# Encoder layer, one core: element-wise sums of the Strassen-Winograd products moved from GpSimd to VectorE, and one pair of steps swapped

## The chip, the cores and the metric

One core of one Trainium2 chip runs the whole program. The metric is the device time of one execution in microseconds (us); lower is better. All arithmetic that matters here is float32; each matmul operand is split into a rounded high part and a low part, and three matmuls (high x high, high x low, low x high) stand for one float32 product.

## The reference

One encoder layer on x (1024 tokens x 1024): a SwiGLU feed-forward block (1024 -> 2 x 2816 -> 1024) as a half step, a mixing block (multi-head latent attention and grouped-query attention, 8 heads each), a second SwiGLU feed-forward block, and a last RMSNorm; scales and shifts come from a vector c through w_ada. The change lies in the two feed-forward blocks:

```
def swiglu(h, w_gu, w_down):
    a, b = jnp.split(h @ w_gu, 2, axis=-1)
    return (jax.nn.silu(a) * b) @ w_down
...
h = modulate(rms_norm(x, g_ffn1[l]), sh_f1, sc_f1)
x = x + 0.5 * gt_f1[:, None, :] * swiglu(h, w1_gu[l], w1_down[l])
```

## The kernel before

The program goes through feed-forward 1 (about 0 to 730 us), attention (to about 1300), the output projection (to about 1390) and feed-forward 2 (to the end). In each feed-forward block h @ w_gu is done by a Strassen-Winograd scheme with seven block products in place of eight. The activations are cut into B11, B21, B12, B22 and their combinations T1 to T4 (`build`, L464); the weights of a unit u of 22 are cut into A11, A12, A22 and their combinations S1 to S4 (`unit_specs`, L416). `prod` (L479) is one block product: 12 matmuls, lines L485, L486 and L487 by turns.

The weights come as a stream (`Stream`, L52): SyncE loads a 1 MB tile `raw` (two buffers); S1 and S3 are made on GpSimd from it (L426), S2 and S4 on VectorE (L426 too); then each block is split: ScalarE makes the high part `uh` (L105), VectorE subtracts it for the low part `ul` (L106). Nine split blocks may be live (`ring`). `pump` (L131) does the next steps of the stream, `get` those that a product needs.

`early2` (feed-forward 2; `early`, L571, does it for 1) and `early_rest` (L550) compute A11 x B11 and then A12 x B21 for units 0 to 7 ahead, since these need no T; between them `builds` makes the T's: eight steps of `build`, in which GpSimd makes T1's first and T3's difference (L468, L473), VectorE the other differences (L470, L476), ScalarE the high parts (L461), and VectorE (T1, T2, T3) or GpSimd (B22, T4) the low parts (L462). A11's product is copied out of its PSUM bank by ScalarE (`c`, L493) before A12's product is added in the same bank.

`run` (L614) then goes through the 22 units, five products for each of the units 0 to 7 and seven for the others. `post` (L495) takes a product out of PSUM on VectorE (L501, L507, L508), with silu on ScalarE, and `g_out` (L512) forms the blocks of g for the down product: the sums S3, S1, S2 and S4 of g on GpSimd (L521), and writes them to DRAM, the A blocks from SyncE's queue and the S blocks from GpSimd's (L517). Behind the last unit the pools are given back, and SyncE loads the gate (L397), x or z (L990, L1610) and the g blocks of the down product (raw<-g_A, L95). In units of feed-forward 1 VectorE also accumulates w_ada (`ada_use`, L313).

The code gives an order by calls; the build then orders each engine's instructions itself by what it reckons to be ready, within data dependences. L313, which the code reaches from unit 8 on, starts at 122.0 us in the trace, between the units 1 and 2. Each engine runs its queue in that order, and waits in it.

Of the kernel before, what the change touches and what calls it, by code (L numbers as in the profile page):

```python
# [19 lines left out]
ALU = mybir.AluOpType  # L20
# [31 lines left out]
class Stream:  # L52
# [87 lines left out]
    def get(self, key):  # L140
        while key not in self.units:
            assert self.i <= self.where[key], key
            if self._next_is_block() and self.live >= RING:
                self.live -= self.freed
                self.freed = 0
                assert self.live < RING, key
            self._step()
        return self.units[key]
# [35 lines left out]
def encoder_layer(ctx: ExitStack, tc: tile.TileContext, a: dict, out: bass.AP):  # L184
    nc = tc.nc
# [10 lines left out]
    st = Stream(nc, rawp, ring)  # L196
# [20 lines left out]
    def small(n, name):  # L217
        return sm.tile([P, 16], F32, tag="small", name=name, bufs=20)[:, 0:n]
# [61 lines left out]
    def ps1():  # L280

        if banks["pair"] is not None:
            p = banks["pair"][:, 512:1024]
            banks["pair"] = None
            return p
        kind = banks["kinds"][banks["n"] % len(banks["kinds"])]
        banks["n"] += 1
        if kind[0] == "2":
            p = ps2()
            if kind == "2":  # L290
                banks["pair"] = p
            return p[:, 0:512]
        return (p0p if kind == "0" else p1p).tile([P, 512], F32, tag="ps1", name="ps1")
# [122 lines left out]
    def unit_specs(i, u, early):  # L416

        src = a[f"w{i}_gu"][u // 2, u % 2]
        A = [slice(j * 512, (j + 1) * 512) for j in range(4)]
        tmps = {}  # L420

        def comb(nm, eng, x, y, op):
            def f(raw):
                tmps[nm] = sp.tile([P, 512], F32, tag="S", name="S")
                get = lambda v: tmps[v] if isinstance(v, str) else raw[:, A[v]]
                eng.tensor_tensor(tmps[nm], get(x), get(y), op=op)  # L426
            return f

        def blk(nm, v):
            if isinstance(v, str):  # L430
                return ((i, u, nm), None, lambda raw: tmps[v])
            return ((i, u, nm), A[v], None)

        direct = not early
        steps = [comb("S1", nc.gpsimd, 2, 3, ALU.add), comb("S3", nc.gpsimd, 0, 2, ALU.subtract)]
        if direct:
            steps.append(blk("A11", 0))
        steps += [comb("S2", nc.vector, "S1", 0, ALU.subtract), blk("S2", "S2"), blk("S1", "S1"), blk("S3", "S3")]
        if direct:
            steps.append(blk("A12", 1))  # L440
        steps += [comb("S4", nc.vector, 1, "S2", ALU.subtract), blk("S4", "S4"), blk("A22", 3)]
        return [(src, steps)]
# [3 lines left out]
    class GateUp:  # L446
# [17 lines left out]
        def build(self, hf, kk, part):  # L464

            b11, b21, b12, b22 = hf[0][:, kk, :], hf[0][:, kk + 4, :], hf[1][:, kk, :], hf[1][:, kk + 4, :]
            if part == 0:
                nc.gpsimd.tensor_tensor(b11, b12, b11, op=ALU.subtract)  # L468
                self.split_b("T1", kk, b11, nc.vector)
                nc.vector.tensor_tensor(b11, b22, b11, op=ALU.subtract)  # L470
                self.split_b("T2", kk, b11, nc.vector)
            else:
                nc.gpsimd.tensor_tensor(b12, b22, b12, op=ALU.subtract)  # L473
                self.split_b("T3", kk, b12, nc.vector)
                self.split_b("B22", kk, b22, nc.gpsimd)
                nc.vector.tensor_tensor(b21, b21, b11, op=ALU.subtract)  # L476
                self.split_b("T4", kk, b21, nc.gpsimd)

        def prod(self, p, u, wn, bn, kks, start, stop):  # L479
            wh, wl = st.get((self.i, u, wn))  # L480
# [31 lines left out]
        def g_out(self, fp, nm):  # L512

            g = self.g

            def put(nm):
                (nc.sync if nm[0] == "A" else nc.gpsimd).dma_start(g_d[nm][:, fp, :], g[nm])  # L517

            def comb(nm, x, y, op, into=None):
                g[nm] = gtp["g"]() if into is None else g[into]  # L520
                nc.gpsimd.tensor_tensor(g[nm], g[x], g[y], op=op)  # L521
                put(nm)

            if nm != "A21":
                put(nm)
            if nm == "A11":
                comb("S3", "A11", "A21", ALU.subtract)
            if nm == "A22":
                comb("S1", "A21", "A22", ALU.add, "A21")
                comb("S2", "S1", "A11", ALU.subtract, "A11")  # L530
                comb("S4", "A12", "S2", ALU.subtract, "A12")
# [18 lines left out]
        def early_rest(self, builds):  # L550

            K4 = (0, 1, 2, 3)
            for u0 in range(NQ0, NE, 4):
                us = range(u0, u0 + 4)
                for u in us:
                    self.bank[u] = ps1()
                    self.prod(self.bank[u], u, "A11", "B11", K4, True, True)
                    self.store_p1(u)
                    next(builds, None)
                    st.pump(2)  # L560
                    bg.step()
                for u in us:
                    self.prod(self.bank[u], u, "A12", "B21", K4, False, True)
                    self.early_out(u)
                    next(builds, None)
                    st.pump(2)
                    bg.step()
            for _ in builds:
                pass
# [96 lines left out]
    def gu_specs(i):  # L666
        for u in range(NU):
            for src, steps in unit_specs(i, u, "rest" if u < NE else None):
                st.add(src, steps)
# [191 lines left out]
    x = [xs.tile([P, D], F32, name=f"x{t}") for t in range(NT)]  # L861
# [121 lines left out]
    x = [dp.tile([P, D], F32, name=f"x{t}") for t in range(NT)]  # L983
# [439 lines left out]
    for s in range(NQ + LAG + 3):  # L1423
        if s < NQ:
            i, t = divmod(s, NT)
            p = scores(i, t)
            nm = small(1, "nm")
            nc.vector.tensor_reduce(nm, p, axis=AX.X, op=ALU.max, negate=True)  # L1428
        b = s - LAG
        if 0 <= b < NQ:  # L1430
            g, e = divmod(b, 2)
# [50 lines left out]
    oT, x, hf = {}, {}, {}  # L1482
# [120 lines left out]
    x = [dp.tile([P, D], F32, name=f"z{t}") for t in range(NT)]  # L1603
# [127 lines left out]
```

## Time and profile before

| | us |
|---|---|
| median of 3 runs | 2048.51 (2046.16 to 2048.94) |
| profiled execution | 2049.28 |
| its span, first to last instruction | 2047.5 |
| TensorE matmul busy in it | 1971.7 (96%), mean granted clock 0.988 |
| VectorE busy | 1540.1 (75%) |
| ScalarE busy | 973.4 (48%) |
| GpSimd busy | 483.7 (24%), 428 instructions |

The profiled execution has its own time, 1.8 us above its span; terms of a sum are taken from its rows. PE stands for TensorE's matmuls, DVE for VectorE, ACT for ScalarE, POOL for GpSimd, SP for SyncE; L106 is line 106 of the kernel before. An arrow in brackets behind a row names what ended the idle time before it.

### The profile page before, as it was taken

What the parts mean: (1) busy time and instruction counts of PE and PEld (TensorE: products, weight loads), DVE (VectorE), ACT (ScalarE), POOL (GpSimd) and SP (SyncE); (2) the same over time, 40 slices, a digit from 0 to 9 for tenths busy, and PEclk for the clock granted to TensorE, in tenths of its full rate; (3) what the DMA queues carried; (4) which work ended last, traced back from release to release, by engine and by line L of the source; (5) the groups of instructions that cost most, each with busy time, mean ns of one, the idle gap of its engine ahead of it and who ended that gap; (6) DMA issues with size and microseconds to landing.
All of it is one profiled execution on the core that took longest, in us unless ns stands there. A gap on an engine that the chain in (4) does not pass through costs nothing. (4 is left out here: it accounts for less than half of the span.)

```text
span 2047.5 us, 28023 instructions
## 1 busy us (share of the span) xinstructions
PE 1971.7 (96%) x10301; PEld 1678.1 (82%) x10301; DVE 1540.1 (75%) x2381; ACT 973.4 (48%) x1865; POOL 483.7 (24%) x428
## 2 busy tenths in 40 slices
PE   6889999999999999999999999998999999999998
PEld 5678888887788888798989998996788888877886
DVE  7898689886697776788888778667776555547976
ACT  6522322322344653677787777467323333324444
POOL 1544344433000032212200000005343332320011
PEclk9999999999999999999999999998999999999999
DMA  8275366565832334523253330433442332358223
GB/s 344 88 246 186 106 202 216 197 223 187 334 116 93 147 123 143 156 63 118 89 165 83 83 75 30 164 127 126 165 163 100 113 118 83 113 207 322 98 93 118
DMA packets 90550, 303.30 MB, mean 148 GB/s; under 512 B 9848, under 2 KB 22427, under 8 KB 76588
## 3 DMA queue, kind: packets, MB, share of 16 engines
q1 hardware_dynamic: 81018, 274.21, 39.8%
q0 software_dynamic: 7040, 23.07, 2.9%
q10 hardware_dynamic: 2354, 4.22, 0.5%
q8 instruction: 81, 1.33, 0.3%
q14 instruction: 57, 0.47, 0.1%
HBM read 220.98 MB, written 80.49 MB: 147 GB/s over the span
## 5 line engine op out<-in xcount | busy, mean ns | idle before, releaser
L105 ACT CAST uh<-raw 128x512 fp32r<-128x512 f32 (+1 forms) x343 | 210.4, 622 | 228.8 <-PE ps L486 148.1
L106 DVE TENSOR_TENSOR ul<-raw,uh 128x512 fp32r<-128x512 f32 (+1 forms) x343 | 250.3, 735 | 41.1 <-ACT uh L105 40.7
L105 ACT CAST uh<-S 128x512 fp32r<-128x512 f32 x198 | 121.6, 621 | 302.3 <-PE ps L486 234.7
L741 PE MATMUL ps<-uh 128*128 128x512 f32 x616 | 240.8, 393 | 7.3 <-ACT uh L105 7.3
L742 PE MATMUL ps<-ul,uh 128*128 128x512 f32 x616 | 241.5, 392 | 1.7 <-DVE ul L106 1.7
L743 PE MATMUL ps<-uh,ul 128*128 128x512 f32 x616 | 240.9, 391 | 0.0
L1428 DVE TENSOR_REDUCE nm<-ps 128x1 f32<-128x1024 f32 x128 | 155.7, 1216 | 70.6 <-PE ps L223 40.9
L106 DVE TENSOR_TENSOR ul<-S,uh 128x512 fp32r<-128x512 f32 x198 | 168.8, 858 | 41.8 <-ACT uh L105 41.6
L521 POOL TENSOR_TENSOR g<-g 128x512 f32<-128x512 f32 x88 | 135.1, 1535 | 244.3 <-DVE g L508 243.3
L1446 ACT CAST ph<-ps 128x512 fp32r<-128x512 f32 x256 | 138.0, 590 | 79.6 <-PE ps L1445 79.4
L426 POOL TENSOR_TENSOR S<-raw 128x512 f32<-128x512 f32 x88 | 123.4, 1414 | 200.3 <-DMA raw<-in_w_gu_dram 122.5
L1456 DVE TENSOR_TENSOR pl<-ps,ph 128x512 fp32r<-128x512 f32 x256 | 163.9, 683 | 0.0
L1451 ACT ACTIVATE pe<-ps,nm 128x1024 f32<-128x1024 f32 x128 | 143.6, 1122 | 17.2 <-DVE nm L1428 17.1
L741 PEld LDWEIGHTS ps<-uh 128*128 128x128 f32 x616 | 116.1, 189 | 33.2 <-ACT uh L105 9.0
L742 PEld LDWEIGHTS ps<-ul,uh 128*128 128x128 f32 x616 | 116.4, 189 | 27.7 <-DVE ul L106 3.8
L743 PEld LDWEIGHTS ps<-uh,ul 128*128 128x128 f32 x616 | 116.3, 189 | 24.2
L1445 PE MATMUL ps<-ident,pe 128*128 128x128 f32 x1024 | 134.9, 273 | 0.8 <-DVE pl L1456 0.4
L1445 PEld LDWEIGHTS ps<-ident,pe 128*128 128x128 f32 x1024 | 119.7, 141 | 19.0 <-DVE pl L1456 0.6
L105 ACT CAST uh<-hT 128x512 fp32r<-128x512 f32 x96 | 59.7, 622 | 150.4 <-PE ps L742 113.5
L1394 PE MATMUL po<-ph,V 128*128 128x256 f32 x512 | 129.7, 291 | 0.0
L1395 PE MATMUL po<-pl,V 128*128 128x256 f32 x512 | 125.9, 283 | 0.0
L233 POOL TENSOR_TENSOR r<-v,neghalf 128x1 f32<-128x1 f32 x32 | 26.0, 813 | 363.8 <-DVE v L229 363.8
(280 smaller groups left out, 5178.0 us busy)
## 6 DMA issues: line engine op xcount, KB each, us to landing
raw<-in_w_gu_dram SPq DMA_DIRECT2D x52, 1024.0 KB
ada<-in_w_ada_dram SPq DMA_DIRECT2D x56, 512.0 KB
g_S<-g POOLq DMA_DIRECT2D x88, 256.0 KB, 2.6
g_A<-g SPq DMA_DIRECT2D x66, 256.0 KB
hT<-in_w_down_dram SPq DMA_DIRECT2D x16, 1024.0 KB
raw<-g_S SPq DMA_DIRECT2D x16, 1024.0 KB
raw<-g_A SPq DMA_DIRECT2D x12, 1024.0 KB
x<-in_x_dram SPq DMA_DIRECT2D x16, 512.0 KB
```

The costliest lines, as they stand in the source:

```text
L105: nc.scalar.copy(hi[:, 0:n], ap)
L106: nc.vector.tensor_tensor(lo[:, 0:n], ap, f32(hi[:, 0:n]), op=ALU.subtract)
L521: nc.gpsimd.tensor_tensor(g[nm], g[x], g[y], op=op)
L741: nc.tensor.matmul(p, gh[:, tsl], wh, start=start, stop=False, skip_group_check=True)
L742: nc.tensor.matmul(p, gh[:, tsl], wl, start=False, stop=False, skip_group_check=True)
L743: nc.tensor.matmul(p, gl[:, tsl], wh, start=False, stop=stop, skip_group_check=True)
L1394: nc.tensor.matmul(po[:, 0:256], V, gr.ph[:, k, :], start=(k == 0), stop=False)
L1428: nc.vector.tensor_reduce(nm, p, axis=AX.X, op=ALU.max, negate=True)
L1445: nc.tensor.transpose(out=pt[:, k, :], in_=pe[:, (4 * n + k) * P:(4 * n + k + 1) * P], identity=ident)
L1446: nc.scalar.copy(gr.ph[:, 4 * n:4 * n + 4, es], pt)
L1451: nc.scalar.activation(pe, p, AF.Exp, bias=nm, accum_out=ls[:, s % 2:s % 2 + 1])
L1456: nc.vector.tensor_tensor(gr.pl[:, nsl, es], pts[n], f32(gr.ph[:, nsl, es]), op=ALU.subtract)
```

## The change

The sums S1 and S3 of the weights, the differences L468 and L473 and the low parts of B22 and T4 in `build`, and the four sums of g in `g_out` are issued on VectorE in place of GpSimd. In `early_rest`, two steps of the weight stream (`pump(2)`) are called ahead of a step of `builds` in place of behind it. GpSimd keeps the DMA issues of g's S blocks (L517).

```diff
@@ -432,7 +432,7 @@
-        steps = [comb("S1", nc.gpsimd, 2, 3, ALU.add), comb("S3", nc.gpsimd, 0, 2, ALU.subtract)]
+        steps = [comb("S1", nc.vector, 2, 3, ALU.add), comb("S3", nc.vector, 0, 2, ALU.subtract)]
@@ -465,16 +465,16 @@
             if part == 0:
-                nc.gpsimd.tensor_tensor(b11, b12, b11, op=ALU.subtract)
+                nc.vector.tensor_tensor(b11, b12, b11, op=ALU.subtract)
                 self.split_b("T1", kk, b11, nc.vector)
...
             else:
-                nc.gpsimd.tensor_tensor(b12, b22, b12, op=ALU.subtract)
+                nc.vector.tensor_tensor(b12, b22, b12, op=ALU.subtract)
                 self.split_b("T3", kk, b12, nc.vector)
-                self.split_b("B22", kk, b22, nc.gpsimd)
+                self.split_b("B22", kk, b22, nc.vector)
                 nc.vector.tensor_tensor(b21, b21, b11, op=ALU.subtract)
-                self.split_b("T4", kk, b21, nc.gpsimd)
+                self.split_b("T4", kk, b21, nc.vector)
@@ -518,7 +518,7 @@
                 g[nm] = gtp["g"]() if into is None else g[into]
-                nc.gpsimd.tensor_tensor(g[nm], g[x], g[y], op=op)
+                nc.vector.tensor_tensor(g[nm], g[x], g[y], op=op)
                 put(nm)
@@ -556,14 +556,14 @@
                     self.store_p1(u)
+                    st.pump(2)
                     next(builds, None)
-                    st.pump(2)
                     bg.step()
...
                     self.early_out(u)
+                    st.pump(2)
                     next(builds, None)
-                    st.pump(2)
                     bg.step()
```

## Rows read from the trace of the kernel before

**Rows 1.** The page, part 1: busy time of each engine.
```profile
PE 1971.7 (96%) x10301; PEld 1678.1 (82%) x10301; DVE 1540.1 (75%) x2381; ACT 973.4 (48%) x1865; POOL 483.7 (24%) x428
```

**Rows 2.** Windows, undisturbed stretch: us, busy (instructions) of PE, PEld, DVE, ACT, POOL, clock, DMA, GB/s.
```profile
1450.00:1500.00 50.00, 50.00 (x222) 41.38 (x222) 36.97 (x49) 15.30 (x25) 18.72 (x16) 1.00 0.46 158
```

**Rows 3.** Waits of PE, whole program: us in total, times, longest.
```profile
PE ps L741 <- ACT uh L105: 7.3, 4, 3.3
PE ps L485 <- ACT c L493: 6.8, 2, 6.2
...
PE ps L487 <- DVE ul L106: 5.7, 3, 3.9
PE ps L485 <- DVE s L501: 4.1, 1, 4.1
```

**Rows 4.** Timelines of DVE, then POOL, in feed-forward 2's early stretch: start, duration, line.
```profile
1398.25 2.65 DVE L106 TENSOR_TENSOR ul<-raw,uh 128x512 fp32r<-128x512 f32 x2 [9.02 <-ACT uh L105]
...
1407.63 0.68 DVE L462 TENSOR_TENSOR T2l<-hT,T2h 128x512 fp32r<-128x512 f32 x1
1408.23 0.68 DVE L462 TENSOR_TENSOR T1l<-hT,T1h 128x512 fp32r<-128x512 f32 x1
...
1411.48 1.79 DVE L106 TENSOR_TENSOR ul<-raw,uh 128x512 fp32r<-128x512 f32 x1
...
1394.86 5.50 POOL L468 TENSOR_TENSOR hT<-hT 128x512 f32<-128x512 f32 x4 [6.41 <-ACT hT L374]
...
1411.05 3.38 POOL L426 TENSOR_TENSOR S<-raw 128x512 f32<-128x512 f32 x2 [3.89 <-DMA raw<-in_w_gu_dram]
```

**Rows 5.** Lines L426 on POOL and L313 on DVE: ns min/median/max, first and last start.
```profile
L426 POOL TENSOR_TENSOR S<-raw x88: 1268/1294/2271, 89.4 to 1767.9; 128x512 f32<-128x512 f32 x88
...
L313 DVE SCALAR_TENSOR_TENSOR acc<-ada,cact,acc x56: 1269/1277/2916, 122.0 to 469.7; 128x1024 f32<-128x1024 f32 x56
```

**Rows 6.** Windows of three stretches, columns as in rows 2.
```profile
100.00:152.00 52.00, 45.60 (x189) 36.65 (x189) 47.21 (x56) 13.51 (x24) 22.71 (x19) 0.94 0.72 248
...
300.00:470.00 170.00, 170.00 (x770) 140.42 (x769) 148.35 (x175) 50.62 (x86) 69.53 (x54) 1.00 0.63 212
...
1396.00:1446.00 50.00, 39.66 (x152) 30.96 (x151) 44.51 (x43) 26.38 (x50) 32.78 (x22) 0.86 0.35 121
```

**Rows 7.** DVE's L313, groups of 108 to 165 us and of 300 to 470 us.
```profile
L313 DVE SCALAR_TENSOR_TENSOR acc<-ada,cact,acc 128x1024 f32<-128x1024 f32 x8 | 12.8, 1594 | 0.0
...
L313 DVE SCALAR_TENSOR_TENSOR acc<-ada,cact,acc 128x1024 f32<-128x1024 f32 x39 | 55.4, 1421 | 8.7 <-DMA ada<-in_w_ada_dram 8.7
```

**Rows 8.** Chain that ended last, end of feed-forward 2's units: start, duration.
```profile
1822.88 1.67 POOL g L521
...
1829.57 3.46 DMA g_S<-g
1833.36 0.33 SPq L397
...
1835.84 10.50 DMA raw<-g_A
```

**Rows 9.** Windows of PE behind it: us, PE busy (instructions), clock, DMA share, GB/s.
```profile
1844.00:1846.00 2.00, 0.30 (x2) 1.00 1.00 411
1846.00:1848.00 2.00, 0.38 (x1) 1.00 1.03 430
1848.00:1850.00 2.00, 1.69 (x6) 0.71 0.38 156
1850.00:1852.00 2.00, 2.00 (x6) 0.50 0.55 102
```

**Rows 10.** Waits of POOL and DVE; then landing of L517's DMAs.
```profile
POOL S L426 <- DMA raw<-in_w_gu_dram: 122.5, 18, 11.7
...
DVE S L426 <- POOL S L426: 17.0, 10, 3.1
...
DMA to landing us min/median/max: 2.3/2.6/8.1
```

## The prediction

> **What bounds the kernel now.** The page comes first: TensorE is busy 96% of the span, VectorE 75%, GpSimd 24% [rows 1]. So only time in which TensorE stands, or runs at the lower clock, can be won. The windows say where that is. An undisturbed 50 us hold 222 matmuls, 0.225 us each [rows 2]. The early stretch of feed-forward 2 holds 152 in 50 us, so 70 x 0.225 = 15.8 us are missing there, and the first units of feed-forward 1 hold 189 in 52 us where 231 would fit, 9.5 us missing; VectorE is busy 89% and 91% of these stretches [rows 6]. The list of waits names what TensorE stood for: low parts of weights (ul, 5.7 us in three waits), the copies c that ScalarE makes (6.8), s of VectorE (4.1), and high parts at the start of the down products (7.3) [rows 3]. Last I read the timelines of the two engines side by side: two operations of VectorE behind each other start 0.60 us apart and take 0.68 each, but one that meets a GpSimd operation takes 1.79 [rows 4]. A GpSimd operation of the same shape takes 1.29 us at the median [rows 5]. GpSimd's help is thus dear: it takes 1.3 us and may cost VectorE 1.1 us, to save VectorE 0.60.
>
> **The price of a moved operation.** 0.60 us of VectorE's queue in place of 0 to 1.11 us (1.79 - 0.68) of standing still. The 1.11 of the row is the most that I book for one. The Trainium skill (SBUF — State Buffer, section "SBUF: two separate sides") says that of two such instructions the later blocks for all of the earlier one. Taken for every instruction, it would put VectorE's time in feed-forward 2's early stretch at 25.8 + 32.8 = 58.6 us of 50, and the gain of that stretch near the whole 15.8; the row of the stretch has 44.5, so the trace does not agree to that extent, and I go by the row.
>
> **Part by part.**
>
> *Feed-forward 2's early stretch, 1396 to 1446 us.* VectorE's 43 operations would take 43 x 0.60 = 25.8 us undisturbed and take 44.5 [rows 6]. The 22 of GpSimd, all moved, add 13.2: 39.0, so 5.5 us less. VectorE also stood 9.02 us until 1398.25, while GpSimd made the four L468 from 1394.86 on [rows 4]; these now start on VectorE itself, 3.4 us earlier. Together 8.9 us in a stretch where VectorE is the engine that is late: c waits in ScalarE's queue behind high parts of T that wait for VectorE's differences. TensorE can win no more than the 15.8 us missing, and nothing if the new order puts the T's in front of what it needs next. I take **-8** (0 to -15.8), near the sum of the rows.
>
> *Feed-forward 1's early stretch, up to 100 us.* Here the swap counts: a unit's weight split gets its place ahead of the T's, on ScalarE and VectorE alike. It aims at the three waits for ul, 5.7 us, and at the slow clock behind them, about 1.0 us by what follows a like gap [rows 3, 9]. The T's pushed behind have the remaining early products to be ready in; if that cover is gone, the start of the units waits for T2 instead. I take **-6** (0 to -6.7), near the far end, since both edits act on the same three waits.
>
> *Feed-forward 1's first units, 100 to 152 us.* At most 8 of the 56 VectorE operations are L313, 1.2 us apart when undisturbed [rows 5, 7]: 8 x 1.2 + 48 x 0.60 = 38.4. Of GpSimd's 19, four DMA issues and a memset stay; 14 moved ones add 8.4: 46.8 us, against 47.2 now [rows 6]. VectorE wins nothing in sum, only the waits of its sums for GpSimd's (3.1 us at the most in one) [rows 10]. I take **-2**; bounds -9.5 (all that is missing) and +5 (VectorE at its limit, four more L313 put in its gaps).
>
> *The two ends of the units.* Behind the last g, three sums run on GpSimd one after another with a DMA issue between, from 1822.88; the last DMA of them starts at 1829.57 and takes 3.46 us; only then do SyncE's loads go out at 1833.36, and behind these the g blocks, which land at 1846.3 [rows 8]. From 1844 to 1852 us TensorE does 15 matmuls where 35.5 fit, 20.5 x 0.225 = 4.6 us: it stands 1.7 + 1.6 + 0.3 = 3.6, then runs at the lower of its two levels (0.50, that is 1.2 GHz; 6 matmuls in 2 us), which costs the other 1.0 [rows 9]. On VectorE the three sums take 1.8 us, 3.6 if a low part is put behind each, so the last DMA starts about 1826.3, 3.3 us earlier. That moves the loads by up to as much; the DMA engines were still at work then, so I count 3.0, nearly the standing time. The end of feed-forward 1 has the same pattern. The three sums also stand in front of the first low parts of the down product: +1.8 us there, against up to 3.3 (three times 1.11) of meetings gone. S2 and S4 of g also overwrite A11 and A12, whose DMAs on SyncE's queue must have read them: on VectorE a late one would now hold those low parts, GpSimd's sums did so at most from 1822.88 on, and I book nothing for it but the lower bound. I take **-6** for both ends (0 to -9.2).
>
> *The remaining units.* From 300 to 470 us VectorE would need 39 x 1.2 + 136 x 0.60 + 33 x 0.60 = 148.2 us (54 of GpSimd less 17 DMA issues and 4 memsets) where it now takes 148.4 of 170 [rows 6, 7]; TensorE is full there. In feed-forward 2's units there is no L313 and more room [rows 2]. What hides the moved work is this room and the nine live blocks of weights. I take **+1** (0 to +6, for posts that come behind the three sums of g).
>
> Sum: -8 - 6 - 2 - 6 + 1 = -21. Against the profiled execution's 2049.3 that is 2028.3; I forecast **2028 us**. That execution lies 0.8 us above the median of 2048.5, which I do not correct for.
>
> **The rivals.**
>
> *VectorE stays the limit.* By the sums above it saves 5.5 us in one stretch and nothing in another, so gains by order alone may be lost to the next late operation: the start of the units, or ScalarE's casts in their queue. Then the two ends and half of the -8 stay, and the ul waits come back elsewhere: 2049.3 - 10 + 1 = 2040. For it speaks that VectorE was already full beside GpSimd; against it, that the waits named are short and few.
>
> *VectorE waits for loads (slower).* GpSimd stood 122.5 us in 18 waits for raw tiles, 6.8 each [rows 10], with nothing useful behind it. On VectorE everything stands behind such a wait: U, s, g, low parts. A unit of five products lasts 13.5 us (60 matmuls) and holds some 17.5 VectorE operations after the move, 10.5 us, so 3.0 are free. If S1 stands 5 us each time, 2.0 us are lost 18 times: 36 us, 2049.3 - 21 + 36 = 2064. It decides from 3.0 + 21/18 = 4.2 us of standing per wait. Against it: S2, on VectorE already, needs the same tile through S1, and stood only 17.0 us in ten waits.
>
> *The S blocks of g go out late.* The DMAs that GpSimd still issues may be held up when VectorE hardly pauses. Today they land in 2.6 us at the median, 8.1 at the most. With 8.1 for the last one the loads would start at 1834.4, later than now: the ends give nothing, 2034. The Trainium skill (SBUF — State Buffer, the same section, its box on DVE and DMA) says that GpSimd cannot write descriptors while VectorE holds the ports they share. The box's case is a copy on both ports, and no run here shows it for sums of two inputs.
>
> **How the numbers follow.** Chances: forecast 0.62, VectorE the limit 0.18, late blocks 0.07, waits for loads 0.13. Cases within 0.2% (4 us, about what a measurement of this kernel can tell from no change) are a third of the second. So faster 0.81, same 0.06, slower 0.13. The bounds of the terms add up to -41 and +11, and do not all fall together; the range takes the forecast with some two thirds of the way down, and up to the limit case with its own play: 2013 to 2045. It leaves out the third rival and the worst of the second.
>
> **What would show it.** Right: no VectorE operation of 128x512 near 1.8 us in the gate-up stretches; the waits PE <- ul and PE <- c shorter; more than 170 matmuls in the 50 us from where T1 starts; L397 some 3 us closer to the last g. Wrong: a row "DVE S <- DMA raw" of tens of us, with PE <- s or g behind it; or VectorE full and TensorE's gaps only moved to the first units; or more L313 among these.

## The result, and the profile after

The kernel after takes 2003.53 us, the median of four runs (2002.6 to 2004.7); the kernel before took 2048.73 us beside it (four runs, 2046.16 to 2049.21). The ratio is 0.9782, with a 95% interval of 0.9765 to 0.9799. The gain is 45 us where 21 were forecast, and the time lies 9.5 us below the lower end of the range. The sign held, and so did the main mechanism, that VectorE and GpSimd hold each other up; the sizes did not, and at the two ends of the units the gain came another way.

The span of the profiled execution fell from 2047.5 to 2000.5 us. Part 1 of the page of the kernel after, which answers to [rows 1]:

```profile
PE 1954.1 (98%) x10301; PEld 1670.9 (84%) x10301; DVE 1554.1 (78%) x2589; ACT 975.0 (49%) x1865; POOL 172.0 (9%) x220
```

VectorE has 208 instructions more. At 0.68 us each they would be 141 us of busy time, yet its sum rose by 14 only: the operations that were there before became shorter. TensorE's busy sum fell with the same 10301 matmuls; its mean granted clock rose from 0.988 to 0.992.

Windows of the kernel after, columns as in [rows 2]. The stretches are those of [rows 6], moved by what had been won ahead of them:

```profile
88.00:140.00 52.00, 51.76 (x228) 42.91 (x229) 50.35 (x79) 17.52 (x31) 3.33 (x5) 1.00 0.67 226
...
280.00:450.00 170.00, 170.00 (x771) 140.67 (x770) 149.97 (x210) 51.43 (x87) 13.03 (x21) 1.00 0.63 213
...
1371.00:1421.00 50.00, 50.00 (x223) 41.34 (x222) 48.81 (x82) 31.41 (x59) 0.00 (x0) 1.00 0.46 158
```

In the early stretch of feed-forward 2, TensorE does 223 matmuls in 50 us instead of 152, and its clock is 1.00 instead of 0.86. The first units of feed-forward 1 hold 228 of the 231 that fit in 52 us. VectorE is 97 to 98% busy there, and TensorE stands for it nowhere in the feed-forward 2 window. VectorE does 82 instructions in the 50 us; before, VectorE's 43 and GpSimd's 22 were 65 together.

The first groups in the list of TensorE's waits after (us in total, times, longest), against [rows 3]:

```profile
PE ps L882 <- DVE v L229: 7.2, 2, 4.3
PE ps L882 <- DVE xn L875: 3.1, 2, 1.6
PE ps L485 <- ACT B11h L461: 3.0, 1, 3.0
...
PE ps L485 <- DVE s L501: 1.9, 1, 1.9
...
PE ps L741 <- ACT uh L105: 0.6, 2, 0.4
```

The waits for the weights' low parts and for c are gone, that for s has halved, and the one at the start of the down products went from 7.3 to 0.6 us. Of the 35.5 us of waits that are left, 20.2 lie in the first 60 us of the program, which the change hardly touches.

L426 in the kernel after (ns min/median/max, first and last start), and what it waited for on VectorE:

```profile
L426 DVE TENSOR_TENSOR S<-raw x88: 679/691/694, 79.4 to 1727.0; 128x512 f32<-128x512 f32 x88
...
DVE S L426 <- DMA raw<-in_w_gu_dram: 16.9, 15, 4.6
```

The longest of 88 sums takes 0.694 us. GpSimd's took 1.29 at the median [rows 5], and VectorE's operations up to 1.79 beside them [rows 4].

To say where the 47 us of span were won, I cut it at starts and ends of TensorE's work: the first product with T2, the first down product, the first input projection of the mixing block, the last output projection, the last product with T4, the last down product. Each number is the length of a section, or, from the second row on, the difference to before in us:

| kernel | to first T2 product | FFN 1 units | FFN 1 down | mixing | FFN 2 gate-up | FFN 2 down |
|---|---|---|---|---|---|---|
| before, length | 98.9 | 399.1 | 221.4 | 661.5 | 439.1 | 217.0 |
| after | -10.7 | -8.1 | -6.2 | +0.1 | -16.0 | -6.8 |
| order alone | -2.9 | +1.6 | -1.3 | +0.1 | -0.1 | +0.2 |
| T alone | -9.4 | -0.9 | -2.6 | +0.1 | -14.8 | +1.0 |
| S alone | +1.6 | -4.7 | -0.5 | +0.1 | -4.3 | -0.2 |
| g alone | +1.6 | -4.2 | -6.1 | 0.0 | +0.3 | -6.8 |

The four rows below "after" are the experiments that follow. Differences of one or two microseconds between single executions carry no weight.

### The profile page after: what moved, and what is told of

The parts are those of the page before. It is cut to its first block, busy times and chain, and to the rows that moved or that the text cites. A ratio compares the mean times of both kernels' runs of the same rounds, so it can differ in the third digit from the quotient of the medians.

```text
span 2000.5 us, 27923 instructions
## 1 busy us (share of the span) xinstructions
PE 1954.1 (98%) x10301; PEld 1670.9 (84%) x10301; DVE 1554.1 (78%) x2589; ACT 975.0 (49%) x1865; POOL 172.0 (9%) x220
## 5 line engine op out<-in xcount | busy, mean ns | idle before, releaser
L106 DVE TENSOR_TENSOR ul<-raw,uh 128x512 fp32r<-128x512 f32 (+1 forms) x343 | 235.4, 692 | 31.5 <-ACT uh L105 31.2
L106 DVE TENSOR_TENSOR ul<-S,uh 128x512 fp32r<-128x512 f32 x198 | 134.5, 684 | 34.4 <-ACT uh L105 34.4
L517 POOL DMA_DIRECT2D g_S<-g x88 | 47.9, 545 | 668.8 <-DVE g L521 597.9
L1394 PEld LDWEIGHTS po<-ph,V 128*128 128x128 f32 x512 | 97.5, 190 | 2.1
L1395 PEld LDWEIGHTS po<-pl,V 128*128 128x128 f32 x512 | 97.8, 191 | 0.2
```

The lines of the kernel that those rows point to most:

```text
L106: nc.vector.tensor_tensor(lo[:, 0:n], ap, f32(hi[:, 0:n]), op=ALU.subtract)
L1394: nc.tensor.matmul(po[:, 0:256], V, gr.ph[:, k, :], start=(k == 0), stop=False)
L1395: nc.tensor.matmul(po[:, 0:256], V, gr.pl[:, k, :], start=False, stop=(k == NT - 1))
```

## Experiments: each part of the change by itself

Four kernels, each the kernel before with one part of the change. Each was compared with the kernel before on the same chip (2047.8 us).

**The order alone**, in both early loops:

```diff
-                    next(builds, None)
                     st.pump(2)
+                    next(builds, None)
                     bg.step()
```

> The kernel before with the swap alone; every sum stays on GpSimd. Theory (VectorE stood behind GpSimd's operations; where these are gone TensorE does not wait): VectorE still meets GpSimd, so of the 45 us only the share that comes from late weight blocks in the early stretches can come: 2 to 6 us faster, about 2045, all of it ahead of the first T2 product. Rival (the new order alone does it): 10 us or more faster, below 2039.

Measured: 2047.51 us, ratio 1.0001 (0.999 to 1.0012). That is under the 2 us that the theory gave at least, and the order is worth nothing that can be told from noise: 1.6 of the 2.9 us at the first T2 product are lost again by the end of the units, and the rest is less than single executions of this kernel differ by.

**T alone:** L468, L473 and the low parts of B22 and T4 on VectorE.

```diff
-                nc.gpsimd.tensor_tensor(b11, b12, b11, op=ALU.subtract)
+                nc.vector.tensor_tensor(b11, b12, b11, op=ALU.subtract)
...
-                self.split_b("T4", kk, b21, nc.gpsimd)
+                self.split_b("T4", kk, b21, nc.vector)
```

> The kernel before with the differences and low parts of the T's on VectorE; S1, S3 and g's sums stay on GpSimd, no swap. Theory: the 26 us that the changed kernel wins ahead of the first T2 product (10.1) and in feed-forward 2's gate-up part (16.0) come mostly from here: 12 to 20 us faster, about 2033, nothing at the two ends of the units. Rival (parts don't add up, order decides): under 6 us.

Measured: 2023.15 us, ratio 0.9878 (0.9857 to 0.9899): 25 us, more than the theory gave (12 to 20) and over half of the whole gain, nearly all of it where the T's are made (-9.4 and -14.8). These are few instructions: 32 of the 208 moved.

**S alone:** S1 and S3 of the weights.

```diff
-        steps = [comb("S1", nc.gpsimd, 2, 3, ALU.add), comb("S3", nc.gpsimd, 0, 2, ALU.subtract)]
+        steps = [comb("S1", nc.vector, 2, 3, ALU.add), comb("S3", nc.vector, 0, 2, ALU.subtract)]
```

> The kernel before with S1 and S3 of the weights on VectorE alone. Theory: the first units of feed-forward 1 and the start of the units in feed-forward 2 win, 4 to 10 us in all, about 2042; VectorE's waits for raw tiles stay under 20 us. Rival (VectorE waits for loads): slower than before, over 2050, with such waits of tens of us.

Measured: 2043.67 us, ratio 0.9975 (0.9964 to 0.9986), 5 us. VectorE waited for raw tiles 22.9 us in 19 waits, 1.2 us each, far from the 4.2 at which the slower rival decides.

**g alone:** the sums of g's blocks.

```diff
-                nc.gpsimd.tensor_tensor(g[nm], g[x], g[y], op=op)
+                nc.vector.tensor_tensor(g[nm], g[x], g[y], op=op)
```

> The kernel before with the four sums of g on VectorE alone. Theory: the two ends of the units win what the changed kernel wins there, 6.2 and 6.7 us from the first down product on, so 10 to 15 us, about 2036, and little ahead of it. Rival (the ends won by the order of SyncE's loads, which the other moves made): under 4 us, and the last load of A12's blocks still behind the gate in SyncE's queue.

Measured: 2034.11 us, ratio 0.9936 (0.9919 to 0.9952): 13 us of span at the two ends, as the whole change has there. The gains of the four by ratio (0, 25, 5 and 13 us) sum to 43 of the 45 us, so the parts add up.

## Experiments: are the meetings the cause?

T and S could have won for either of two reasons: VectorE and GpSimd hold each other up, or a chain of steps is quicker on one engine. Two kernels test the first. Both are the kernel after, with extra work on GpSimd beside each of the 120 T and S operations that had moved; nothing takes its result, and both give up one of six scratch tiles for it. The first makes a sum of the same operands:

```diff
+    def beside(x, y):
+        nc.gpsimd.tensor_tensor(dmy, x, y, op=ALU.add)
...
                 self.split_b("T4", kk, b21, nc.vector)
+                beside(b21, f32(self.Bh["T4", kk]))
```

> The kernel after, and beside each weight sum (S1, S3) and each T operation that came over to VectorE GpSimd makes an extra 128x512 sum of the same operands into a tile that nobody reads; no data waits on it (a block's buffer comes free only when GpSimd has read it too). One of the scratch tiles of the norms is given up for its output. Blocking theory (VectorE's and GpSimd's two-input operations hold each other up; most of the 45 us came from those meetings): VectorE's operations beside GpSimd's sums take about 1.8 us again in place of 0.68, and since VectorE keeps the added work too, most of the 30 us that T's and S's gave are lost: 2025 to 2060 us. Rival (the gain came from the chain being on one engine, without handing over to GpSimd whose operation takes 1.28 us and without its queue): the extra sums are on no chain, 2001 to 2009 us.

The second, the control, fills the same tile and reads one column:

```diff
+        nc.gpsimd.memset(dmy, 0.0)
+        nc.gpsimd.tensor_tensor(dmy[:, 0:1], x[:, 0:1], y[:, 0:1], op=ALU.add)
```

> The control of the run before: in place of each extra sum GpSimd fills the same tile with zeros (128x512, no operand to read) and reads one column of the two operands. Both theories: GpSimd is about as busy, reads next to nothing, and the time stays within 5 us of the kernel after (2000 to 2009 us), with VectorE's 128x512 operations near 0.68 us. If it lost as much as the extra sums do, it would be GpSimd's holding the blocks, or its writes, and not its reading beside VectorE.

Measured: 2058.5 us with the sums, ratio to before 1.0057 (1.0042 to 1.0072), and 2007.52 us with the fills, ratio 0.9807 (0.979 to 0.9823). The sums cost 51 us more than the fills. Against the kernel after, the execution with the sums is 15.9 us later at the first T2 product, 20.0 longer in feed-forward 1's units and 20.6 in feed-forward 2's gate-up part; both down parts are within 0.1 us. That is where the added sums are, and nowhere else.

The longest wait of TensorE in the gate-up parts, with the sums, then with the fills, is the one in front of the first T2 product (us in total, times, longest):

```profile
PE ps L496 <- issue: 14.4, 1, 14.4
```

```profile
PE ps L497 <- POOL dmy L200: 3.9, 1, 3.9
```

For the 14.4 us the profile names no releaser ("issue"); the 3.9 it puts down to a fill. So some 10 of the 51 us may come from the place of the extra instructions in the queues and not from slower operations of VectorE. Another 5 are VectorE standing until GpSimd had read a block (3.9 and 1.2 us). The rest, about 35 us, is still more than the 30 that T and S won together. The meetings alone are thus enough for that gain; what a shorter chain adds to it was not separated.

The low parts of T4 in the kernel with the sums, then with the fills (ns min/median/max, first and last start):

```profile
L469 DVE TENSOR_TENSOR T4l<-hT,T4h x4: 683/1754/1778, 1429.4 to 1451.2; 128x512 fp32r<-128x512 f32 x4
```

```profile
L470 DVE TENSOR_TENSOR T4l<-hT,T4h x4: 684/685/689, 1391.3 to 1404.0; 128x512 fp32r<-128x512 f32 x4
```

Timelines of the kernel with the sums in this stretch, VectorE, then GpSimd (start, duration):

```profile
1427.04 0.68 DVE L478 TENSOR_TENSOR hT<-hT 128x512 f32<-128x512 f32 x1
...
1430.05 0.68 DVE L519 TENSOR_TENSOR eg<-ps,es 128x512 f32<-128x512 f32 x1
1430.65 1.17 DVE L106 TENSOR_TENSOR ul<-raw,uh 128x512 fp32r<-128x512 f32 x1
1431.74 1.78 DVE L469 TENSOR_TENSOR T3l<-hT,T3h 128x512 fp32r<-128x512 f32 x1
1433.44 1.77 DVE L469 TENSOR_TENSOR B22l<-hT,B22h 128x512 fp32r<-128x512 f32 x1
1435.13 1.74 DVE L486 TENSOR_TENSOR hT<-hT 128x512 f32<-128x512 f32 x1
1436.80 0.68 DVE L469 TENSOR_TENSOR T3l<-hT,T3h 128x512 fp32r<-128x512 f32 x1
...
1426.62 4.65 POOL L200 TENSOR_TENSOR dmy<-hT,B22h 128x512 f32<-128x512 f32 x1 [10.88 <-DVE ul L106]
1431.34 1.63 POOL L200 TENSOR_TENSOR dmy<-hT,T4h 128x512 f32<-128x512 f32 x1
1433.05 1.61 POOL L200 TENSOR_TENSOR dmy<-hT 128x512 f32<-128x512 f32 x1
1434.74 1.59 POOL L200 TENSOR_TENSOR dmy<-hT,B22h 128x512 f32<-128x512 f32 x1
```

From 1431.7 on the two engines take turns: VectorE starts an operation every 1.69 us and GpSimd one every 1.70. A pair costs 1.70 us; VectorE alone would make both in 2 x 0.60 = 1.20, by its undisturbed spacing. Where both have work, GpSimd's help thus makes the pair slower than VectorE is by itself. The Trainium skill (SBUF — State Buffer, section "SBUF: two separate sides") says that of two such instructions the first to start shuts the other out for its whole length, and only where GpSimd's reads SBUF. These rows, and the control beside them, agree.

Windows of the 50 us that begin 15 us after the mixing block's last product, in the kernel with the sums, then with the fills:

```profile
1407.00:1457.00 50.00, 37.13 (x144) 28.76 (x144) 48.82 (x51) 23.93 (x45) 34.84 (x20) 0.90 0.27 95
```

```profile
1374.00:1424.00 50.00, 48.62 (x211) 38.99 (x210) 44.69 (x74) 30.34 (x57) 21.51 (x35) 1.00 0.46 158
```

VectorE is busy 48.8 us of 50 with 51 instructions in the one, and 44.7 us with 74 in the other. TensorE does 144 matmuls against 211.

**The order, undone in the kernel after** (a weight's split behind the T's again):

```diff
-                    st.pump(2)
                     next(builds, None)
+                    st.pump(2)
                     bg.step()
```

> The kernel after without the change of order in the early units (a weight's split comes behind the T's again); all sums and low parts on VectorE. By the runs of the parts (the order alone gave nothing, the parts sum to 43 of 45 us): 2002 to 2007 us. Rival (with the T's on VectorE the order decides who waits: the T's come first in VectorE's queue and TensorE waits for the weight's low part): 2008 to 2016 us, with the first T2 product some us later or earlier.

Measured: 2002.15 us (2001.57 to 2002.89), ratio 0.9781 (0.9766 to 0.9795): no difference that this measurement can tell from the kernel after. The order is worth nothing with the T's on VectorE either.

## Experiment: what won the two ends

The gate's load (L397) was to go out some 3 us closer to the last g. SyncE's queue at the end of feed-forward 2's units, in the kernel before, then after:

```profile
1833.36 0.33 SPq L397 DMA_DIRECT2D gate<-gd  x1
1833.74 1.99 SPq L1610 DMA_DIRECT2D z<-xd  x4
1835.84 1.11 SPq L95 DMA_DIRECT2D raw<-g_A  x2
```

```profile
1786.74 0.33 SPq L95 DMA_DIRECT2D raw<-g_A  x1
1793.52 0.33 SPq L397 DMA_DIRECT2D gate<-gd  x1
1793.90 1.96 SPq L1610 DMA_DIRECT2D z<-xd  x4
```

The gate did not come closer: it stands 11.3 us behind the start of the last L508 before (1822.1) and 12.3 after (1781.2). Its wait in both kernels is for the S blocks of g. The last DMA of these, before, then after:

```profile
L517 POOL DMA_DIRECT2D g_S<-g x1: 557/557/557, 1829.6 to 1829.6; - x1
...
DMA to landing us min/median/max: 3.5/3.5/3.5
```

```profile
L517 POOL DMA_DIRECT2D g_S<-g x1: 539/539/539, 1785.9 to 1785.9; - x1
...
DMA to landing us min/median/max: 7.4/7.4/7.4
```

The sums did come out sooner: this DMA starts 4.7 us behind the start of the last L508, 7.5 before. But it takes 3.9 us longer to land, and the gate's load goes out when it has landed (1833.0 and 1793.3). Why it took longer was not tried.

The gain came by another load: one of g's blocks now stands ahead of the gate. It starts 7.6 us behind the start of the last product with T4 (1779.1), where before the first started 15.8 us behind (1820.0). The diff doesn't touch these lines; the order on SyncE's queue came out differently when the kernel was built. The end of feed-forward 1 has the same: raw at 485.63 and gate at 491.34 after, gate at 511.43 and raw at 513.89 before. Every kernel here with g's sums on VectorE has the load ahead, the one with g alone too; the kernels with the order, T or S alone have it behind.

So I took the kernel before and moved nothing but loads, at the end of both feed-forward blocks (the cut shows the first), with every sum and low part where it was:

```diff
-    gate = bcast_row(dp, gd[0], "gate")
+    gate = bcast_row(dp, gd[0], "gate", nc.gpsimd)
...
-            nc.sync.dma_start(x[t], a["x"][t * P:(t + 1) * P, :])
+            nc.gpsimd.dma_start(x[t], a["x"][t * P:(t + 1) * P, :])
```

> The kernel before, with the gate's load and the eight loads of x (or z) at the end of each FFN put on GpSimd's queue, so that on SyncE's queue the last blocks of g and the down weights no longer stand behind them; sums, low parts and the early units' order as before. Theory (the two ends were won by the order of SyncE's loads): the first product of the unit after the gate-up part no longer waits for its weight (7.3 us before), each end gives 4 to 7 us, 2034 to 2041 us. Rival (the ends were won by g's sums coming out sooner on VectorE): 2045 to 2049 us.

Measured: 2040.9 us, ratio 0.9969 (0.9958 to 0.9981), just inside what the theory gave. The down parts take 5.1 and 4.7 us less, against 6.2 and 6.8 in the kernel after, and the 7.3 us of waits at their start are down to 0.4. SyncE's queue and a window of TensorE in this kernel:

```profile
1818.41 0.49 SPq L86 DMA_DIRECT2D hT<-in_w_down_dram  x1
1823.24 6.25 SPq L95 DMA_DIRECT2D raw<-g_A  x2
```

```profile
1806.00:1856.00 50.00, 49.21 (x215) 39.74 (x214) 32.59 (x47) 19.44 (x35) 12.59 (x17) 1.00 0.88 340
```

The like windows of the kernel before and after (each begins 9 us ahead of the last product with T4):

```profile
1811.00:1861.00 50.00, 45.32 (x189) 35.96 (x188) 28.91 (x42) 16.62 (x31) 7.82 (x8) 0.97 0.79 300
```

```profile
1770.00:1820.00 50.00, 49.73 (x218) 40.61 (x218) 33.09 (x54) 19.97 (x36) 2.17 (x4) 1.00 0.86 330
```

189 matmuls before, 215 with the loads moved, 218 after. The order of the loads alone can thus give three quarters of what the ends gave, (5.1 + 4.7) of (6.2 + 6.8) us. The edit also brings loads of the down weights forward; how much is theirs and how much the g blocks', and whether the rest is the quicker sums, was not tried.

## Why the prediction was wrong in size

**What bounds the kernel: right.** Only TensorE's standing and slow time could be won. The mixing block, which the change leaves alone, kept its length to 0.1 us.

**Feed-forward 2's early stretch, -8 forecast, -16.0 measured for the gate-up part (T alone -14.8): the step that failed most.** The 15.8 us missing in [rows 6] are two things. TensorE stood for 50 - 39.7 = 10.3 us, and its 152 matmuls took 39.7 us in place of 152 x 0.225 = 34.2, another 5.5. The slow matmuls stand right behind the long waits. Windows of the kernel before (columns as in [rows 2]), the first behind the wait of 6.2 us for c, the second behind a wait of 3.0 for ScalarE's es:

```profile
1423.00:1429.00 6.00, 6.00 (x14) 4.74 (x15) 6.00 (x6) 2.21 (x5) 4.12 (x4) 0.50 0.73 250
1442.00:1446.00 4.00, 4.00 (x11) 3.13 (x12) 0.90 (x3) 0.00 (x0) 1.48 (x2) 0.58 0.72 277
```

The forecast took the 8.9 us that it had added up for VectorE as TensorE's gain. That is near the 10.3 of standing; the slow matmuls behind it were put at nothing here, though they were counted at the two ends. Both came back whole and together (223 matmuls, clock 1.00). The 8.9 itself left out a wait, since standing is not busy time: VectorE stood 3.1 us for a weight sum of GpSimd. It is the second of these rows (kernel before, 1396 to 1446 us); the first is the one that the forecast saw:

```profile
DVE ul L106 <- ACT uh L105: 9.0, 1, 9.0
DVE S L426 <- POOL S L426: 3.1, 1, 3.1
```

By the rule of the Trainium skill (the section named above), which I set aside, the gain was near the whole 15.8. That this figure came out is luck as far as its working goes: it had all 43 operations of VectorE held (58.6 us), and of these 18 took 1.66 to 1.79 us and 24 took 0.68 or 0.69. The low parts of T4, first and last start, before (on GpSimd) and after:

```profile
L462 POOL TENSOR_TENSOR T4l<-hT,T4h x4: 1622/1702/1742, 1418.5 to 1432.2; 128x512 fp32r<-128x512 f32 x4
```

```profile
L462 DVE TENSOR_TENSOR T4l<-hT,T4h x4: 682/684/694, 1388.0 to 1398.0; 128x512 fp32r<-128x512 f32 x4
```

From the mixing block's last product (1380.9 and 1356.0) to the start of the last of them: 51.3 us before, 42.0 after, 9.3 less.

**Feed-forward 1's early stretch, -6 forecast, -10.7 measured.** "Here the swap counts" is refuted: the order alone gave 2.9 us there and nothing in the whole, and undoing it in the kernel after cost nothing. The T's gave 9.4. The place was right. TensorE's waits and a window of it, from 60 us to the first T2 product, before, then the waits after:

```profile
PE ps L487 <- DVE ul L106: 5.4, 2, 3.9
PE ps L485 <- ACT uh L105: 0.8, 1, 0.8
PE ps L485 <- ACT es L502: 0.8, 1, 0.8
...
60.00:98.90 38.90, 31.92 (x130) 24.58 (x129) 34.87 (x36) 26.42 (x48) 21.83 (x14) 0.96 0.22 77
```

```profile
PE ps L485 <- issue: 1.1, 1, 1.1
```

The bound of 6.7 left out the waits for uh and es, 1.6 us, and put the slow clock at 1.0, where the 130 matmuls took 31.9 us in place of 130 x 0.225 = 29.3, 2.7 more. Some 2 us were won ahead of 60 us. With the order alone the waits for ul fell to 2.2 us, but TensorE then stood 2.7 us in front of the first T2 product: the loss of cover that the prediction named as the risk of the swap.

**The first and the remaining units of feed-forward 1, -2 and +1 forecast, -8.1 measured.** The 9.5 us missing are 6.4 of standing (52 - 45.6) and 3.1 of slow matmuls (45.6 - 189 x 0.225), and the -2 allowed for neither in full. "VectorE wins nothing in sum" speaks of its busy time alone; VectorE also stood 4.2 us in three waits for weight sums of GpSimd in the kernel before (98.9 to 152 us), all gone after:

```profile
DVE S L426 <- POOL S L426: 4.2, 3, 2.5
```

Nearly all of the 9.5 came back there (228 of 231 matmuls); the wait of 1.9 us for s that is left comes later, at 185 us. S alone gave 4.7 in this section and g alone 4.2.

**The two ends, -6 forecast, -13.0 measured.** The place was right, the cause wrong. The step that failed is "That moves the loads by up to as much": counted from the last L508, the last of the S blocks was issued 2.8 us sooner (3.3 were forecast), but its DMA took 3.9 us longer and the gate's load went out 1.0 us later. A load that no longer stood behind the gate gave most of the gain instead. The bound of 4.6 us an end was too small, since I looked at 8 us from 1844 on. In the 50 us from 1811, 33 matmuls are missing against the undisturbed 222, 33 x 0.225 = 7.4 us.

**The rivals.** *VectorE stays the limit*: it is 97% busy in the stretch and TensorE is full, so no. *VectorE waits for loads*: 16.9 us in 15 waits, 1.1 each against the 4.2 at which it decides, and TensorE's full windows leave no room for a wait behind them. *The S blocks go out late*: in part, yes. Over all 88 DMAs the landing changed little,

```profile
DMA to landing us min/median/max: 2.3/2.9/8.9
```

0.3 us more at the median than before [rows 10]. But the last one of feed-forward 2 took 7.4 us, near the 8.1 of this rival, and that is why the gate's load came no sooner. The ends won all the same, since a load of g's blocks stood ahead of it; as far as the forecast goes, that was luck.

**The signs named ahead.** No VectorE operation near 1.8 us in the gate-up stretches, waits for ul and c gone, 223 matmuls where over 170 were named: all came. L397 closer by 3 us did not.

## What to carry to other kernels

Split what TensorE lacks in a stretch into standing and slow matmuls before pricing it: a third of it was the second here (5.5 of 15.8 us, 3.1 of 9.5), and it came back with the first. Don't read room from an engine's busy share: blocked operations count as busy (1.7 us in place of 0.68), and its standing can be waits for the very partner that the change removes (3.1 and 4.2 us here). Two-input sums on GpSimd beside a busy VectorE are worth less than nothing here (1.70 us a pair against 1.20); stretches where VectorE has time to spare were not tried. And a queue's order can change where the diff is silent: compare the load queue of both traces before giving a gain to the lines that were edited.

## What the chip showed that was not expected

A sum on GpSimd can be held far longer than one operation of VectorE: the one at 1426.62 took 4.65 us, while VectorE ran six of its operations at its undisturbed spacing of 0.60 us, and the longest of this kind took 6.46. A fill on GpSimd, a write with nothing to read, took 0.53 us and left VectorE's 128x512 sums at 0.69.
